# A Strassen SwiGLU stage: weight blocks loaded three column tiles ahead, with fewer pages for each tile

## Chip, cores and metric

The kernel runs on one core of one Trainium2 chip. The metric is the device time of one execution in microseconds (us), as the median of several runs of the same kernel. The profile is of one execution.

## The reference

One block of a diffusion backbone: 512 tokens of width 1024, and 256 context tokens. A mixing part (chunkwise retention and latent attention, merged by gates) is followed by a gated SwiGLU network of hidden width 2816. Everything is float32. The change lies in the first half of the network, where h is 512 x 1024 and w_gu 1024 x 5632:

```python
def _swiglu(h, w_gu, w_down):
    a, b = jnp.split(h @ w_gu, 2, axis=-1)
    return (jax.nn.silu(a) * b) @ w_down
```

## The kernel before, in words

**Numbers in two parts.** Every product in float32 is made of three matmuls (`mm3`, lines 121 to 123). Each operand is split into a high part, rounded by ACT (`split`, line 105), and a low part, the difference, which DVE makes (line 106).

**Tiles.** The hidden width is 22 tiles of 128 columns, each with a gate block and an up block of w_gu, 128 x 1024 each. Tiles 0 to 2 are computed plainly (`early_mm`). Tiles 3 to 21, 19 of them, go through the class `Hidden`, in Strassen's way: a 2 x 2 scheme over halves of the features and halves of the tokens with seven products instead of eight, `p1` to `p7`, in the order p1, p5, p2, p6, p3, p7, p4. A product is 12 matmuls of 128 x 128 weights on 256 columns, so a tile takes 84. The products p1, p6, p7 and p4 add up in one PSUM place, gy, and between them the running value is copied or added out: qz (line 1003, ACT), ub (line 1018, ACT), the sum of line 1027 (DVE), and lines 1031 and 1032 (DVE), which finish the tile. p5 and p3 add up in gz (line 1008, ACT, and line 1022, DVE), and p2 stands alone in gx (line 1013, DVE). Two neighbouring tiles, an even and an odd one, share a gy. The scheduler draws a piece of the next product between two products into gy.

**Operands of a tile.** `loads` brings four blocks. The first half of the up block goes twice into s13, by two transfers on SP's queue (lines 959, 960). The raw gate block goes into a ring of three raw buffers (`load`, line 110, SP). The second half of the up block, wgb, goes into a page (line 963, SP). Then POOL issues two accumulating transfers which add a further half to each half of s13 in memory (lines 964, 965). `sums` makes s24 from s13 and the raw block by two additions on DVE (lines 969, 970). Then the four splits follow: `split_a` (the raw block, into a ring of three weight buffers, "w"), `split_13`, `split_24` and `split_22` (into pages). There are 29 pages of 128 x 1024 words for everything.

**What sets the order.** Each engine and each queue works in order. The code is written step by step (the loop over f at the end of the stage) and a scheduler merges the steps into one order for each engine; waits follow from the data and from the buffers. In the loop, the loads of tile f+2 and its sums are written behind p6 of tile f, split_13 and split_24 of f+1 around p5 of f, and split_a of f+2 behind p3. Before the loop, the feature halves hx are combined into t1 to t4 (`combine`), each in a page of its own, and split as the moving operands T1 to T4. Behind the stage comes the projection with w_dn, whose raw blocks and splits use the same two rings.

Of the kernel before, what the change touches and what calls it, by code (L numbers as in the profile page):

```python
# [18 lines left out]
F32R = mybir.dt.float32r  # L19
BF16 = mybir.dt.bfloat16  # L20
AF = mybir.ActivationFunctionType
ALU = mybir.AluOpType
# [4 lines left out]
P = 128  # L27
# [36 lines left out]
def block(ctx: ExitStack, tc: tile.TileContext, xc, xtok, crow, wada, bada, w_rg, w_rv, w_rqk, w_kv, w_dq,  # L64
          w_gr, w_gm, w_ro, dec, ncol, w_qk, w_v, w_mo, w_out, lnrow, w_gu, w_dn, rtab, ktab, qtab, out):
    nc = tc.nc
    V, S, G, T = nc.vector, nc.scalar, nc.gpsimd, nc.tensor
# [3 lines left out]
    whl = ctx.enter_context(tc.tile_pool(name="whl", bufs=3))  # L71
# [10 lines left out]
    def nm(s):  # L82
        uid[0] += 1
        return f"{s}{uid[0]}"

    def page(shape, dt=F32, n="pg"):
        return pgp.tile(shape, dt, tag="pg", name=nm(n))

    def eight(shape, dt=F32, n="e8"):
        return e8p.tile(shape, dt, tag="e8", name=nm(n))  # L90

    def half(shape, dt=F32, n="hp"):
        return hpp.tile(shape, dt, tag="hp", name=nm(n))
# [4 lines left out]
    def bank(n="ps"):  # L98
        return pss.tile([P, 512], F32, tag="ps", name=nm(n))
# [4 lines left out]
    def split(h, l, src):  # L104
        S.copy(h, src)  # L105
        V.tensor_tensor(l, src, h.bitcast(F32), ALU.subtract)  # L106

    def load(ap, n):
        t = wraw.tile([P, 1024], F32, tag="wr", name=nm("wr"))
        nc.sync.dma_start(t[:, :n], ap)  # L110
        return t

    def weight(ap, n=1024):
        r = load(ap, n)
        w = whl.tile([P, 2, 1024], F32R, tag="w", name=nm("w"))
        split(w[:, 0, :n], w[:, 1, :n], r[:, :n])
        return w
# [55 lines left out]
    for ft in range(KT):  # L173
        if ft + 2 < KT:
            first_loads(ft + 2)
        bs, bh, r, xp = first[ft]
# [5 lines left out]
        h = eight([P, 2, NL], F32R, "hL")  # L182
# [5 lines left out]
        w = whl.tile([P, 2, 1024], F32R, tag="w", name=nm("w"))  # L188
        split(w[:, 0], w[:, 1], r)
        for n in range(8):  # L190
            c = slice(n * P, (n + 1) * P)
# [99 lines left out]
    def feat_mm(o, st, mv, ktn=KT):  # L291
        for k in range(ktn):
            mm3(o, st(k), mv(k), k == 0, k == ktn - 1)
# [232 lines left out]
    def run(g):  # L526
        for _ in g:
            pass
# [161 lines left out]
    for n in range(8):  # L690
        retention_out(n)
        if n == KN:
# [11 lines left out]
            sums = page([64, NL], n="sums")  # L704
# [9 lines left out]
    w = weight(w_v)  # L714
    m = row_max(0)
    vt = []
    for t in range(NTA):
# [4 lines left out]
        for f in range(2):  # L722
            if t < NTL:
                st = ck[f][:, 0, t * P:(t + 1) * P], ck[f][:, 1, t * P:(t + 1) * P]
            else:
                c = slice((t - NTL) * P, (t - NTL + 1) * P)
# [130 lines left out]
    hx, hb = {}, {}  # L857
# [69 lines left out]

    def combine(a, b, op, n):  # L930
        t = page([P, 4, 256], n=n)
        V.tensor_tensor(t, a, b, op)
        return t

    def moving(src, n, neg=False):
        a, b = eight([P, 4, 256], F32R, n + "h"), eight([P, 4, 256], F32R, n + "l")
        if neg:
            S.activation(a, src, AF.Copy, scale=-1.0)
            V.scalar_tensor_tensor(b, src, -1.0, a.bitcast(F32), ALU.mult, ALU.subtract)
        else:  # L940
            split(a, b, src)
        return a, b

    def product(o, st, mv, more=False):
        for k in range(4):
            c = slice(k * P, (k + 1) * P)
            mm3(o, (st[0][:, c], st[1][:, c]), (mv[0][:, k], mv[1][:, k]), k == 0 and not more, k == 3, more)

    class Hidden:
# [6 lines left out]
        def loads(self):  # L956
            ga, gb = w_gu[2 * self.f], w_gu[2 * self.f + 1]
            s = self.s13 = page([P, 2, 512], n="s13")
            nc.sync.dma_start(s[:, 0], gb[:, :512])
            nc.sync.dma_start(s[:, 1], gb[:, :512])  # L960
            self.a = load(ga, 1024)
            self.b = page([P, 512], n="wgb")
            nc.sync.dma_start(self.b, gb[:, 512:])
            G.dma_start(s[:, 0], gb[:, 512:], accum_op=ALU.add)  # L964
            G.dma_start(s[:, 1], ga[:, :512], accum_op=ALU.add)
# [8 lines left out]
            split(w[:, 0], w[:, 1], self.a)  # L974
            self.a11, self.a12 = [(w[:, 0, c], w[:, 1, c]) for c in (slice(0, 512), slice(512, 1024))]

        def halves(self, s, n):
            a, b = page([P, 2, 512], F32R, n + "h"), page([P, 2, 512], F32R, n + "l")
            split(a, b, s)
            return [(a[:, i], b[:, i]) for i in range(2)]  # L980

        def split_13(self):
            self.s1, self.s3 = self.halves(self.s13, "s13")

        def split_24(self):
            self.s2, self.s4 = self.halves(self.s24, "s24")

        def split_22(self):
            w = page([P, 2, 512], F32R, "a22")
# [35 lines left out]
        def p7(self):  # L1025
            product(self.y, self.s3, T3, True)
            V.tensor_tensor(self.ub[:, 1], self.y, self.qz[:, 1], ALU.add)

        def p4(self):
            product(self.y, self.a22, T4, True)  # L1030
            V.scalar_tensor_tensor(self.o[:, :256], self.y, -1.0, self.o[:, :256], ALU.mult, ALU.mult)
            V.scalar_tensor_tensor(self.o[:, 256:], self.ub[:, 1], -1.0, self.o[:, 256:], ALU.mult, ALU.mult)

    def steps(f, names):
        if f in hid:
            for n in names.split():
                getattr(hid[f], n)()

    ys = {}
    hid = {f: Hidden(f) for f in range(NEARLY, FT)}  # L1040

    def early_mm(f, tp):
        c = slice(tp * 256, tp * 256 + 256)
        pab = []
        for s in range(2):
            ps = bank("gu")
            feat_mm(ps[:, :256], wg[2 * f + s], lambda k: (hb[k // 4, tp][0][:, k % 4], hb[k // 4, tp][1][:, k % 4]))
            pab.append(ps[:, :256])
        sa = half([P, 256], n="sa")
        S.activation(sa, pab[0], AF.Silu)  # L1050
        V.tensor_tensor(tv[f // 2][:, f % 2, c], pab[1], sa, ALU.mult)
# [4 lines left out]
    F0 = NEARLY  # L1056
    for f in range(NEARLY):
        early_mm(f, 0)
    steps(F0, "loads")
    run(ln)  # L1060
    t1 = combine(hx[0, 0], hx[0, 1], ALU.subtract, "t1")
    q = combine(hx[1, 1], t1, ALU.add, "t2")
    early_mm(0, 1)
    T1 = moving(t1, "t1")
    steps(F0, "split_a split_13")
    early_mm(1, 1)
    T2 = moving(q, "t2", True)
    steps(F0, "sums split_24")
    steps(F0 + 1, "loads")
    for f in range(2, NEARLY):  # L1070
        early_mm(f, 1)
    T3 = moving(combine(hx[1, 1], hx[0, 1], ALU.subtract, "t3"), "t3")
    B11, B21, B22 = hb[0, 0], hb[1, 0], hb[1, 1]
    steps(F0, "p1")
    steps(F0 + 1, "split_a")
    steps(F0, "p5")
    T4 = moving(combine(q, hx[1, 0], ALU.subtract, "t4"), "t4")
    steps(F0, "p2 split_22 p6")
    steps(F0 + 1, "split_13 sums")
    steps(F0, "p3 p7")  # L1080
    steps(F0 + 1, "split_24")
    steps(F0 + 2, "loads")
    for f in range(F0 + 1, FT):
        steps(f, "p1")
        if f == F0 + 1:
            steps(f, "split_22")
            steps(f + 1, "sums split_a")
        steps(f + 1, "split_13")
        steps(f, "p5")
        steps(f + 1, "split_24")  # L1090
        steps(f, "p2")
        steps(f + 1, "split_22")
        steps(f, "p6")
        steps(f + 2, "loads sums")
        steps(f, "p3")
        steps(f + 2, "split_a")
        steps(f - 1, "p4")
        steps(f, "p7")
    steps(FT - 1, "p4")


# [39 lines left out]
    for k in range(FT):  # L1141
        w = weight(w_dn[k])
# [16 lines left out]
    for k in range(FT - NLATE):  # L1159
        w = weight(w_dn[k])  # L1160
# [34 lines left out]
    for k in range(FT - NLATE, FT):  # L1195
        r = load(w_dn[k], 1024)
        a = page([P, 1024], F32R, "wdh")
        b = page([P, 1024], F32R, "wdl")
# [119 lines left out]
```

## Time and profile before

| what | us |
|---|---|
| median of three runs | 1021.82 (1020.51 to 1023.26) |
| the profiled execution's own time | 1018.94 |
| its span in the profile | 1017.2 |
| the Strassen stage, tiles 3 to 21 | 226.3 |

The profile gives for each engine what it did and what it waited for. A timeline row reads: start, duration, engine and line, operation with its output and inputs, and in brackets the idle time before it with what ended it. "SPq" and "POOLq" are the instructions that issue transfers. PE is TensorE, DVE is VectorE, ACT is ScalarE. In the windows, an engine's busy time stands with its number of instructions in brackets, then the granted clock of TensorE as a share of the full one, the busy share of the DMA engines and the rate.

### The profile page before, as it was taken

The page shows a single profiled execution, that of the slowest core. Times are in us where ns is not written, and L with a number is a line of the kernel's source. Part 1 is how long each engine was busy: PE and PEld are TensorE (multiplying, and loading weights), DVE is VectorE, ACT ScalarE, POOL GpSimd, SP SyncE. Part 2 cuts the span into 40 slices and gives each one's busy share as a digit, 9 for nine tenths or more (in the row PEclk, how much of TensorE's full clock was granted, in tenths as well). Part 3 has the DMA queues.
Part 4 walks back from the last instruction along what each step waited for, and adds up shares of the span by engine and source line. Part 5 has one row for each costly group of instructions (what it writes and reads, how often), then busy time and mean ns, then how long its engine had stood idle before and what let it go on. Part 6 is the DMA issues. An engine that isn't in the chain of part 4 may idle for free. (4 is left out here: it accounts for less than half of the span.)

```text
span 1017.2 us, 13877 instructions
## 1 busy us (share of the span) xinstructions
PE 959.8 (94%) x5384; PEld 815.0 (80%) x5384; DVE 702.0 (69%) x1096; ACT 447.2 (44%) x686; POOL 76.8 (8%) x115
## 2 busy tenths in 40 slices
PE   5999999999999998999999989979899988999995
PEld 3888888888899786776766769978789988988884
DVE  6959877537753665788886867755667664794946
ACT  3344253323333531377676544434444442653341
POOL 0000100100011010000000001011112111000002
PEclk9999999999999999999999999999999998999998
DMA  9746511111034578510003576256667666576771
GB/s 356 310 132 233 211 63 42 42 57 47 22 116 144 164 218 248 125 42 22 1 2 124 181 218 206 82 142 148 162 175 179 157 164 146 187 248 196 216 227 44
DMA packets 52467, 147.49 MB, mean 145 GB/s; under 512 B 8113, under 2 KB 9265, under 8 KB 52401
## 3 DMA queue, kind: packets, MB, share of 16 engines
q1 hardware_dynamic: 39456, 123.62, 37.4%
q0 software_dynamic: 6112, 11.54, 7.2%
q10 hardware_dynamic: 6832, 11.45, 3.4%
q8 instruction: 42, 0.69, 0.3%
q14 instruction: 25, 0.20, 0.1%
HBM read 140.81 MB, written 4.20 MB: 143 GB/s over the span
## 5 line engine op out<-in xcount | busy, mean ns | idle before, releaser
L105 ACT CAST w<-wr 128x1024 fp32r<-128x1024 f32 (+2 forms) x137 | 141.4, 1033 | 194.4 <-PE wd L123 49.0
L106 DVE TENSOR_TENSOR w<-wr,w 128x1024 fp32r<-128x1024 f32 (+2 forms) x137 | 164.0, 1198 | 83.0 <-ACT w L105 82.9
L122 PE MATMUL wd<-w,tt 128*128 128x512 f32 (+1 forms) x163 | 61.0, 374 | 0.0
L121 PE MATMUL wd<-w,tt 128*128 128x512 f32 (+1 forms) x163 | 60.8, 374 | 0.0
L123 PE MATMUL wd<-w,tt 128*128 128x512 f32 (+1 forms) x163 | 60.8, 373 | 0.0
L121 PE MATMUL gt<-hL,w 128*128 128x512 f32 x128 | 50.9, 398 | 0.2 <-DVE ck L484 0.2
L122 PE MATMUL gt<-hL,w 128*128 128x512 f32 x128 | 50.7, 396 | 0.0
L123 PE MATMUL gt<-hL,w 128*128 128x512 f32 x128 | 50.7, 396 | 0.0
L149 DVE SCALAR_TENSOR_TENSOR junk<-wr,sc 128x1024 bf16<-128x1024 f32 x20 | 24.4, 1222 | 27.2 <-DMA wr<-in_wada_dram 26.5
L105 ACT CAST s13h<-s 128x1024 fp32r<-128x1024 f32 x19 | 19.9, 1047 | 51.8 <-DMA s<-in_w_gu_dram 51.8
L405 POOL TENSOR_SCALAR sm<-sm 128x1 f32<-128x1 f32 x18 | 8.8, 486 | 426.1 <-DVE sm L825 349.2
L106 DVE TENSOR_TENSOR s13l<-s,s13h 128x1024 fp32r<-128x1024 f32 x19 | 23.3, 1224 | 24.2 <-ACT s13h L105 24.2
L123 PEld LDWEIGHTS wd<-w,tt 128*128 128x128 f32 x163 | 30.7, 188 | 5.9
L121 PEld LDWEIGHTS wd<-w,tt 128*128 128x128 f32 x163 | 30.6, 188 | 5.9
L122 PEld LDWEIGHTS wd<-w,tt 128*128 128x128 f32 x163 | 30.6, 188 | 5.9
L106 DVE TENSOR_TENSOR pt<-ex,pt 128x512 fp32r<-128x512 f32 x48 | 30.7, 685 | 4.0 <-ACT pt L105 4.0
L614 DVE TENSOR_REDUCE sm<-sc 128x1 f32<-128x768 f32 x32 | 29.7, 952 | 2.4 <-PE sc L613 2.2
L969 DVE TENSOR_TENSOR s<-s,wr 128x512 f32<-128x512 f32 x19 | 13.1, 689 | 26.2 <-DMA s<-in_w_gu_dram 26.2
L964 POOL DMA_DIRECT2D s<-in_w_gu_dram x19 | 16.7, 876 | 189.5 <-DMA s<-in_w_gu_dram 64.1
L511 ACT ACTIVATE gate<-gt 128x512 f32<-128x512 f32 x16 | 9.6, 598 | 48.6 <-PE gt L123 48.6
L121 PE MATMUL gy<-t2h,s24h 128*128 128x256 f32 x76 | 22.5, 296 | 7.5 <-ACT qz L1003 7.5
L121 PEld LDWEIGHTS gt<-hL,w 128*128 128x128 f32 x128 | 24.1, 188 | 6.0 <-DVE ck L484 0.5
(438 smaller groups left out, 3144.1 us busy)
## 6 DMA issues: line engine op xcount, KB each, us to landing
wr<-in_w_dn_dram SPq DMA_DIRECT2D x44, 512.0 KB, 3.7
wr<-in_w_gu_dram SPq DMA_DIRECT2D x25, 512.0 KB, 3.5
wr<-in_wada_dram SPq DMA_DIRECT2D x20, 512.0 KB, 4.0
s<-in_w_gu_dram SPq DMA_DIRECT2D x38, 256.0 KB, 3.9
s<-in_w_gu_dram POOLq DMA_DIRECT2D x38, 256.0 KB, 4.5
wr<-in_w_out_dram SPq DMA_DIRECT2D x16, 512.0 KB, 4.3
ada_m<-in_wada_dram SPq DMA_DIRECT2D x12, 512.0 KB, 5.8
wgb<-in_w_gu_dram SPq DMA_DIRECT2D x19, 256.0 KB, 4.3
```

Of the source, the lines that this page charges most:

```text
L105: S.copy(h, src)
L106: V.tensor_tensor(l, src, h.bitcast(F32), ALU.subtract)
L121: T.matmul(o, st[0], mv[0], start=start, stop=False, skip_group_check=more)
L122: T.matmul(o, st[0], mv[1], start=False, stop=False, skip_group_check=more)
L123: T.matmul(o, st[1], mv[0], start=False, stop=stop, skip_group_check=more)
L149: V.scalar_tensor_tensor(junk, raw, 1.0, vec, ALU.mult, ALU.mult, accum_out=acc[:, b:b + 1])
L405: G.tensor_scalar(dst, src, scale, eps, ALU.mult, ALU.add)
L511: S.activation(dst[n // 2][:, n % 2], ps, AF.Sigmoid)
L614: V.tensor_reduce(mx[:, t:t + 1], ps.rearrange("p a b -> p (a b)")[:, :NA], AX.X, ALU.max)
L964: G.dma_start(s[:, 0], gb[:, 512:], accum_op=ALU.add)
L969: V.tensor_tensor(s[:, 0], self.s13[:, 0], self.a[:, :512], ALU.add)
```

## The change

- The loads of a tile are written three tiles ahead instead of two: those of f+3 behind p1 of f.
- `split_13` puts its two parts into the weight ring (name w13) instead of two pages. The ring keeps three buffers and now has two users.
- wgb of an even and an odd tile share one page.
- The differences t1 to t4 of the features are written over the halves hx that they are made from, so `combine` and its pages go.
- The steps stand in another order: split_24 of f+1 ahead of p2, split_13 of f+1 behind p2, sums of f+2 behind p6, split_a of f+2 behind p7, split_22 of a tile in its own round behind p5.

```diff
--- before.py
+++ after.py
@@ -927,11 +927,6 @@
 
 
 
-    def combine(a, b, op, n):
-        t = page([P, 4, 256], n=n)
-        V.tensor_tensor(t, a, b, op)
-        return t
-
     def moving(src, n, neg=False):
         a, b = eight([P, 4, 256], F32R, n + "h"), eight([P, 4, 256], F32R, n + "l")
         if neg:
@@ -959,7 +954,9 @@
             nc.sync.dma_start(s[:, 0], gb[:, :512])
             nc.sync.dma_start(s[:, 1], gb[:, :512])
             self.a = load(ga, 1024)
-            self.b = page([P, 512], n="wgb")
+            if self.f // 2 not in bs:
+                bs[self.f // 2] = page([P, 2, 512], n="wgb")
+            self.b = bs[self.f // 2][:, self.f % 2]
             nc.sync.dma_start(self.b, gb[:, 512:])
             G.dma_start(s[:, 0], gb[:, 512:], accum_op=ALU.add)
             G.dma_start(s[:, 1], ga[:, :512], accum_op=ALU.add)
@@ -974,16 +971,15 @@
             split(w[:, 0], w[:, 1], self.a)
             self.a11, self.a12 = [(w[:, 0, c], w[:, 1, c]) for c in (slice(0, 512), slice(512, 1024))]
 
-        def halves(self, s, n):
-            a, b = page([P, 2, 512], F32R, n + "h"), page([P, 2, 512], F32R, n + "l")
-            split(a, b, s)
-            return [(a[:, i], b[:, i]) for i in range(2)]
-
         def split_13(self):
-            self.s1, self.s3 = self.halves(self.s13, "s13")
+            w = whl.tile([P, 2, 1024], F32R, tag="w", name=nm("w13"))
+            split(w[:, 0], w[:, 1], self.s13.rearrange("p a b -> p (a b)"))
+            self.s1, self.s3 = [(w[:, 0, c], w[:, 1, c]) for c in (slice(0, 512), slice(512, 1024))]
 
         def split_24(self):
-            self.s2, self.s4 = self.halves(self.s24, "s24")
+            a, b = page([P, 2, 512], F32R, "s24h"), page([P, 2, 512], F32R, "s24l")
+            split(a, b, self.s24)
+            self.s2, self.s4 = [(a[:, i], b[:, i]) for i in range(2)]
 
         def split_22(self):
             w = page([P, 2, 512], F32R, "a22")
@@ -1036,7 +1032,7 @@
             for n in names.split():
                 getattr(hid[f], n)()
 
-    ys = {}
+    ys, bs = {}, {}
     hid = {f: Hidden(f) for f in range(NEARLY, FT)}
 
     def early_mm(f, tp):
@@ -1058,44 +1054,48 @@
         early_mm(f, 0)
     steps(F0, "loads")
     run(ln)
-    t1 = combine(hx[0, 0], hx[0, 1], ALU.subtract, "t1")
-    q = combine(hx[1, 1], t1, ALU.add, "t2")
+    t1, t3, q, t4 = hx[0, 0], hx[0, 1], hx[1, 1], hx[1, 0]
+    V.tensor_tensor(t1, hx[0, 0], hx[0, 1], ALU.subtract)
+    V.tensor_tensor(t3, hx[1, 1], hx[0, 1], ALU.subtract)
+    V.tensor_tensor(q, hx[1, 1], t1, ALU.add)
     early_mm(0, 1)
     T1 = moving(t1, "t1")
     steps(F0, "split_a split_13")
+    steps(F0 + 1, "loads")
     early_mm(1, 1)
     T2 = moving(q, "t2", True)
     steps(F0, "sums split_24")
-    steps(F0 + 1, "loads")
+    steps(F0 + 2, "loads")
     for f in range(2, NEARLY):
         early_mm(f, 1)
-    T3 = moving(combine(hx[1, 1], hx[0, 1], ALU.subtract, "t3"), "t3")
+    T3 = moving(t3, "t3")
+    V.tensor_tensor(t4, q, hx[1, 0], ALU.subtract)
     B11, B21, B22 = hb[0, 0], hb[1, 0], hb[1, 1]
     steps(F0, "p1")
+    steps(F0 + 3, "loads")
     steps(F0 + 1, "split_a")
-    steps(F0, "p5")
-    T4 = moving(combine(q, hx[1, 0], ALU.subtract, "t4"), "t4")
-    steps(F0, "p2 split_22 p6")
-    steps(F0 + 1, "split_13 sums")
+    steps(F0, "p5 p2 split_22 p6")
+    steps(F0 + 1, "sums")
+    T4 = moving(t4, "t4")
+    steps(F0 + 1, "split_13 split_24")
     steps(F0, "p3 p7")
-    steps(F0 + 1, "split_24")
-    steps(F0 + 2, "loads")
+    steps(F0 + 1, "split_22")
+    steps(F0 + 2, "sums split_a")
     for f in range(F0 + 1, FT):
         steps(f, "p1")
-        if f == F0 + 1:
+        steps(f + 3, "loads")
+        steps(f, "p5")
+        if f > F0 + 1:
             steps(f, "split_22")
-            steps(f + 1, "sums split_a")
-        steps(f + 1, "split_13")
-        steps(f, "p5")
         steps(f + 1, "split_24")
         steps(f, "p2")
-        steps(f + 1, "split_22")
+        steps(f + 1, "split_13")
         steps(f, "p6")
-        steps(f + 2, "loads sums")
+        steps(f + 2, "sums")
         steps(f, "p3")
-        steps(f + 2, "split_a")
         steps(f - 1, "p4")
         steps(f, "p7")
+        steps(f + 2, "split_a")
     steps(FT - 1, "p4")
```

The first place is SP's queue in the middle of the stage. s13 is the sum block of a tile, wr its raw gate block, wgb its second up half; before, the rows are these:

```order
L110 DMA wr1043_6232<-in_w_gu_dram 128x1024
L959 DMA s131012_5981<-in_w_gu_dram 128x512
L960 DMA s131012_5981<-in_w_gu_dram 128x512
L963 DMA wgb1014_5986<-in_w_gu_dram 128x512
L110 DMA wr1059_6357<-in_w_gu_dram 128x1024
L959 DMA s131028_6106<-in_w_gu_dram 128x512
L960 DMA s131028_6106<-in_w_gu_dram 128x512
L963 DMA wgb1030_6111<-in_w_gu_dram 128x512
L110 DMA wr1073_6480<-in_w_gu_dram 128x1024
L959 DMA s131042_6229<-in_w_gu_dram 128x512
L960 DMA s131042_6229<-in_w_gu_dram 128x512
```

and with the change:

```order
L110 DMA wr1013_6052<-in_w_gu_dram 128x1024
L110 DMA wr1025_6173<-in_w_gu_dram 128x1024
L954 DMA s131024_6170<-in_w_gu_dram 128x512
L955 DMA s131024_6170<-in_w_gu_dram 128x512
L960 DMA wgb1026_6175<-in_w_gu_dram 128x512 x2
L954 DMA s131039_6294<-in_w_gu_dram 128x512
L955 DMA s131039_6294<-in_w_gu_dram 128x512
L110 DMA wr1040_6297<-in_w_gu_dram 128x1024
L110 DMA wr1052_6418<-in_w_gu_dram 128x1024
L954 DMA s131051_6415<-in_w_gu_dram 128x512
```

Before, the raw block of a tile stands right ahead of the s13 loads of the tile two before it (wr1043 belongs to the same tile as s131042, in the last row but one). With the change the raw block and the s13 loads of one tile stand together (wr1025 and s131024), the wgb loads of two tiles follow each other, and the loads of two tiles stand side by side.

The second place is DVE's queue from the sum of p2 of an even tile to the sum of p7 of the same tile, on which p1 of the odd tile waits (L1027 before, L1023 with the change). Before:

```order
L1013 TENSOR_TENSOR tv1078_6534<-gx1085_6571,qz1079_6535 128x256
L1022 TENSOR_TENSOR tv1078_6534<-gz1082_6553,ub1087_6588 128x256
L106 TENSOR_TENSOR a221086_6585<-wgb1074_6482,a221086_6585 128x512
L1031 SCALAR_TENSOR_TENSOR tv1048_6286<-gy1047_6285,tv1048_6286 128x256
L1027 TENSOR_TENSOR ub1087_6588<-gy1077_6533,qz1079_6535 128x256
L1032 SCALAR_TENSOR_TENSOR tv1078_6534<-ub1087_6588,tv1078_6534 128x256
L969 TENSOR_TENSOR s241091_6611<-s131088_6602,wr1089_6605 128x512
L970 TENSOR_TENSOR s241091_6611<-s241091_6611,wr1089_6605 128x512
```

and with the change (the line numbers are four lower there, and three for the sums):

```order
L1009 TENSOR_TENSOR tv1091_6769<-gx1099_6813,qz1092_6770 128x256
L966 TENSOR_TENSOR s241102_6844<-s131078_6660,wr1079_6663 128x512
L106 TENSOR_TENSOR w131100_6827<-s131066_6539,w131100_6827 128x1024
L967 TENSOR_TENSOR s241102_6844<-s241102_6844,wr1079_6663 128x512
L106 TENSOR_TENSOR a221109_6928<-wgb1053_6420,a221109_6928 128x512
L1018 TENSOR_TENSOR tv1091_6769<-gz1095_6792,ub1101_6830 128x256
L106 TENSOR_TENSOR s24l1111_6932<-s241102_6844,s24h1110_6931 128x1024
L1027 SCALAR_TENSOR_TENSOR tv1064_6524<-gy1063_6523,tv1064_6524 128x256
L966 TENSOR_TENSOR s241115_6966<-s131093_6784,wr1094_6787 128x512
L1023 TENSOR_TENSOR ub1101_6830<-gy1090_6768,qz1092_6770 128x256
L967 TENSOR_TENSOR s241115_6966<-s241115_6966,wr1094_6787 128x512
```

The sum of p7 is the row whose output is ub1087, and ub1101 with the change. Before, the two additions for a later tile (L969, L970) stand behind it. With the change the first addition for the tile three further on (L966, s241115) stands ahead of it, and so do both additions for the tile before that one (s241102), with the splits w131100, a221109 and s24l1111. On TensorE, five matmuls of p5 of the odd tile stood between p7 of the even tile and p1 of the odd one; with the change there are eight.

## Rows read from the trace of the kernel before

**Rows 1.** The page: its first line, the span and the instructions of the execution.

```profile
span 1017.2 us, 13877 instructions
```

**Rows 2.** Windows: start:end, length, busy us by engine, PEclk, DMA share, GB/s.

```profile
659.30:885.60 226.30, 201.74 (x1604) 196.05 (x1603) 141.11 (x214) 99.12 (x160) 30.99 (x36) 0.98 0.64 162
760.00:780.00 20.00, 19.37 (x163) 19.15 (x162) 14.56 (x22) 9.74 (x15) 3.49 (x4) 1.00 0.73 183
850.00:859.00 9.00, 6.89 (x35) 6.89 (x36) 4.94 (x6) 4.86 (x8) 1.67 (x2) 0.62 0.52 164
```

**Rows 3.** The same window, instructions of gy, gz and gx alone (PE first).

```profile
659.30:885.60 226.30, 120.66 (x907) 113.19 (x907) 15.17 (x37) 14.00 (x38) 0.98 0.64 162
...
659.30:885.60 226.30, 64.34 (x456) 58.90 (x456) 7.91 (x19) 7.02 (x19) 0.98 0.64 162
...
659.30:885.60 226.30, 31.01 (x228) 29.11 (x228) 7.96 (x19) 0.98 0.64 162
```

**Rows 4.** Timeline: start, us, engine, line, operation [idle before, and releaser].

```profile
775.17 0.28 PE L122 MATMUL gy<-t3l,s13h 128*128 128x256 f32 x1
...
776.59 0.28 PE L122 MATMUL gz<-t1l,s13h 128*128 128x256 f32 x1
...
777.03 0.41 DVE L1027 TENSOR_TENSOR ub<-gy,qz 128x256 f32<-128x256 f32 x1
...
777.50 0.39 PE L121 MATMUL gy<-hbh,w 128*128 128x256 f32 x1 [0.63 <-DVE ub L1027]
```

**Rows 5.** Waits of PE in 659.3 to 885.6: us in total, times, longest.

```profile
PE gy L121 <- ACT qz L1003: 7.5, 4, 3.1
PE gy L121 <- ACT ub L1018: 6.0, 5, 1.7
PE gy L121 <- DVE ub L1027: 3.9, 4, 1.3
PE gz L121 <- ACT s13h L105: 3.5, 2, 3.1
PE gz L121 <- ACT qz L1008: 2.1, 2, 1.5
```

**Rows 6.** Waits of SP's queue in 659.3 to 885.6.

```profile
SPq L110 <- DVE s L970: 142.9, 16, 14.1
```

**Rows 7.** Timeline: one round of loads, and the first raw load of the count.

```profile
669.71 0.33 SPq L110 DMA_DIRECT2D wr<-in_w_gu_dram  x1
...
835.50 0.33 SPq L110 DMA_DIRECT2D wr<-in_w_dn_dram  x1
...
836.25 1.04 ACT L105 CAST s13h<-s 128x1024 fp32r<-128x1024 f32 x1 [5.59 <-DMA s<-in_w_gu_dram]
...
838.15 0.36 ACT L1003 COPY qz<-gy 128x256 f32<-128x256 f32 x1
...
838.57 0.38 PE L121 MATMUL gy<-t2h,s24h 128*128 128x256 f32 x1 [2.61 <-ACT qz L1003]
...
840.10 0.42 SPq L960 DMA_DIRECT2D s<-in_w_gu_dram  x1
...
843.44 1.22 POOL L965 DMA_DIRECT2D s<-in_w_gu_dram  x1
...
848.55 0.33 SPq L110 DMA_DIRECT2D wr<-in_w_dn_dram  x1
...
850.74 1.04 ACT L105 CAST s13h<-s 128x1024 fp32r<-128x1024 f32 x1 [7.64 <-DMA s<-in_w_gu_dram]
```

**Rows 8.** DMA issues on the page: count, KB each, median us to landing.

```profile
s<-in_w_gu_dram SPq DMA_DIRECT2D x38, 256.0 KB, 3.9
s<-in_w_gu_dram POOLq DMA_DIRECT2D x38, 256.0 KB, 4.5
```

**Rows 9.** DVE's groups in 700 to 880: busy us, mean ns, idle before.

```profile
L106 DVE TENSOR_TENSOR w<-wr,w 128x1024 fp32r<-128x1024 f32 x15 | 18.3, 1217 | 0.0
L969 DVE TENSOR_TENSOR s<-s,wr 128x512 f32<-128x512 f32 x15 | 10.4, 690 | 23.5 <-DMA s<-in_w_gu_dram 23.5
```

## The prediction

> **What bounds the kernel now.** I read the windows first, then the waits of TensorE, then the queue of SP, and last one round of loads in the timeline. The span is 1017.2 us [rows 1]. The changed stage runs from the first Strassen matmul of tile 3 to the last of tile 21, 659.30 to 885.60, so 226.3 us with 1604 matmuls [rows 2]. Of these, 907 + 456 + 228 = 1591 write gy, gz and gx [rows 3]; the 13 others are the first of the projection behind. Inside an undisturbed run the matmuls start 0.118 us apart: the rows at 775.17 and 776.59 are twelve matmuls apart, 1.42 us [rows 4]. So 1591 matmuls need 188.2 us, or 84 x 0.118 = 9.92 us a tile. The 13 others are 512 columns wide; at twice the spacing they take 3.1 us. That leaves 226.3 - 188.2 - 3.1 = **35.0 us in which TensorE is held up**, and this is all that the change can win there.
>
> Where are these 35.0 us? The five largest groups of TensorE's waits come to 7.5 + 6.0 + 3.9 + 3.5 + 2.1 = 23.0 us [rows 5]. All but one name a copy or sum that takes a product out of PSUM (lines 1003, 1008, 1018, 1027). The mean granted clock of the stage is 0.98, so about 0.02 x 226.3 = 4.5 us more; it falls to 0.62 in 850 to 859, right behind a pause of TensorE [rows 2]. The rest is small.
>
> The releasers named are quick instructions, though; the question is why they were late. The round in rows 7 tells it. TensorE starts p6 at 838.57 after 2.61 us idle, for the copy of line 1003. ACT starts that copy at 838.15, because the casts of that round stand ahead of it in its queue, and the first of them began at 836.25, after ACT had idled 5.59 us for the DMA of s13. So the sum block was late, and ACT, in order, took the evacuation down with it.
>
> Why was the block late? SP waits 142.9 us in the stage, 16 times, with the raw load (line 110) for the second addition of the sums, line 970 [rows 6]. The raw ring has three buffers, so the raw block of tile f+2 waits until tile f-1's is read; and in SP's order the two loads of s13 of tile f stand behind it. The raw load (here already one of w_dn) goes at 835.50, the second load of s13 at 840.10, the accumulating transfers are issued by POOL until 843.44, the cast behind them begins at 850.74, and the next raw load goes at 848.55 only [rows 7]. This is a closed loop, one turn for each tile. Added up from its rows: three issues on SP 0.33 + 0.33 + 0.42 (the first s13 load taken like the raw one), landing 3.9 [rows 8], POOL's issue 1.22 [rows 7], landing of the accumulate 4.5 [rows 8], two additions of 0.69 [rows 9]: 12.1 us. Measured it is (848.55 - 669.71) / 16 turns = **11.18 us** [rows 7], against the 9.92 that TensorE needs. The loop, not TensorE, sets the pace: 19 x (11.18 - 9.92) = 23.9 us, which is about the 23.0 of the waits.
>
> **The change, part by part.**
> Loads three tiles ahead. SP's raw load of tile f now waits for the ring to be read by split_a and the sums of f-3, and the s13 loads wait for pages freed by p3 and p4 of f-5 and f-6. In SP's new order the loads of a tile stand together. The turn thus goes over three tiles, with 12.1 us of transfers in it against some 2 x 9.92 = 19.8 us between the issue and the first use (line 966 of the same tile). It leaves about 8 us to spare. Every wait for the s13 DMA goes. What is late next is DVE, below. Can the queues carry it? A tile moves seven times 256 KB, 1.84 MB in 9.92 us, 185 GB/s; the stretch 760 to 780 had 183 GB/s with the DMA engines busy to 0.73 and TensorE 19.37 of 20 us [rows 2]. Yes.
>
> The raw split in the weight ring. The sums of s13 now take one of three ring buffers instead of two pages. Two users share the ring: split_13 of f+1 waits for p2 of f, split_a of f+2 for p7 of f. Both are needed only products later, so I take nothing in the stage; at the end, the first split of the next projection waits until the last p6 has read the ring. That cast and subtraction (about 1.0 + 1.22 [rows 9]) lie partly beside the last two products (2 x 12 x 0.118 = 2.8 us): bounds 0 and 2.2, I take 1.0.
>
> wgb in shared pages, differences in place. Neither adds an instruction in the loop. Pages per tile fall from 8 to 5.5, which is what lets three tiles be in flight. In place, t3 is made earlier than before: two more wide DVE operations stand among the splits ahead of p1 of tile 3. Bounds 0 and 2 x 1.22 = 2.4 by the nearest row [rows 9]; they have other matmuls of the early tiles over them, so I take 0.5. If that cover were gone, it would be 2.4.
>
> The new order on DVE. This is the term that stays. Products of one pair of tiles write the same gy, and p1 of the odd tile waits until DVE has added p7 of the even one (line 1023, before line 1027); the wait is 0.63 to TensorE in the row at 777.50, which starts 0.47 after the sum began at 777.03 [rows 4]. Now eight matmuls of p5 lie between p7 and p1, before it was five: 0.35 us more cover. But in front of line 1023 the queue holds, from p2's end: line 1009, line 966, w13l, 967, a22l, 1018, s24l, 1027, line 966 of the next tile, so 0.41 + 0.69 + 1.22 + 0.69 + 0.69 + 0.41 + 1.22 + 0.41 + 0.69 = 6.4 us by [rows 4, 9]. A matmul lasts 0.28, 0.16 beyond its slot [rows 4]; so, counted from p2's last slot, this is done at 6.6, and TensorE restarts 0.47 after line 1023's start, 7.1. TensorE itself comes to p1 after p6, p3, p4, p7 and 8 of p5, 56 x 0.118 = 6.6. The wait is 0.5 by full durations; back-to-back instructions on DVE overlap by up to a tenth, so the lower end is 0. I take 0.25, plus 0.1 for p7 of the odd tile behind the sum of p4: 0.35 for a pair, 9 pairs, **3.2 us**; bounds 0 and 5.4 (0.6 x 9).
>
> Sum: of the 35.0 us, 3.2 + 0.5 + 1.0 = 4.7 stay; 30.3 go. The profiled execution took 1018.94 us, so 988.6; the median of the runs, 1021.82, lies 2.9 above it, so **991 us** in their scale. If all 35.0 went it would be 983.9, or 986.8; I set the low end at 985.
>
> A rule against this. The rows show 3.9 and 4.5 us from issue to landing for 256 KB [rows 8], and 7.3 between the second POOL issue and the cast behind it [rows 7]. With these the turn is over 9.92. The Trainium skill, page "DMA: Bandwidth & Descriptors", section "Anatomy of one DMA — SWDGE (gpsimd) path", gives about 2.0 us plus bytes over 436 GB/s for such a transfer, so an estimate of 2.6 us; by it a turn would be 8.9 us, shorter than a tile's matmuls, the loads would hold nobody, and earlier loads would win nothing. The trace disagrees: the rows say 4.5 and the measurement decides.
>
> **The rivals.**
> (a) DVE becomes the bound. If one more 1024-wide half, w of split_a, falls in front of line 1023 in each pair, 1.22 us more are lost there: 9 x 1.22 = 11.0. For it: DVE is busy 14.56 of 20 us when TensorE runs full [rows 2], and is in order. Against: split_a comes behind line 1023 in its order. The gain is then 19.3 and the time 1002. Chance 0.13.
> (b) The loads are not the cause, or the loop only moves: the transfers land in a burst and the raw ring, still of three, keeps the pace at 11.18. A loop whose turn is short without contention, as reckoned from rows by less than 9.92, would be the same case. For it: the ring did not grow. Against: SP's 142.9 us wait is for line 970, which has a tile more time now. Time 1018 to 1022. Chance 0.06.
> (c) Slower. In DVE's new order line 966 of a tile three ahead stands in front of line 1023. A late accumulate would then hold the evacuation of p7, and TensorE, directly, and no longer ACT's copies alone. It decides when issue to landing passes some 20 us; the longest turn in rows, 835.50 to 850.74, is 15.2. Loads of two tiles now leave together, 3.7 MB; at the 183 GB/s of [rows 2] that is 20 us. To be slower it must cost more than 35.0 / 19 = 1.84 us a tile; at 2.4 it is 19 x 2.4 = 45.6, 10.6 more than now, 1032. Chance 0.03, as the queues had 0.27 of their time free in that stretch.
>
> **How the numbers follow.** The forecast has 0.78: 991, alone 985 to 997 (with the upper bounds 5.4 + 2.4 + 2.2 = 10.0 left in the stage, 25.0 go: 993.9, or 996.8). Case (a) adds 0.13 up to 1002. I give 985 to 1002, which leaves out (b), (c) and a little of either end. About 0.3% (3 us) is what a measurement of this kernel can tell from no change. Faster by more than that: 0.78 + 0.13 = 0.91; the same, case (b): 0.06; slower, (c): 0.03.
>
> **What would show it.** In the changed profile the stage should last about 196 us (193 without the 13 others) with a granted clock of 1.00. ACT's wait for the s13 DMA should be gone, raw loads on SP should go at 10 us spacing, and TensorE's waits should come to some 5 us, led by gy waiting for the sum of line 1023. If raw loads still go every 11 us, (b) is right; if gy waits for line 1023 over 1 us a pair, (a); if line 966 idles for the DMA, (c). Should the stage fall as forecast but the span not, a stage behind it lost what this one won.

## The result, and the profile after

The changed kernel takes 994.56 us (median of four runs, 991.36 to 995.30) against 1021.38 us (median of four). The ratio of the runs is 0.9729, 95% interval 0.9703 to 0.9755; that of the two medians is 0.9737. The forecast was 991 us, in a range of 985 to 1002. Measured again later beside the kernel before (e10), the same kernel took 991.79 against 1019.27, 0.9732 (0.9706 to 0.9759). Two of the four executions of experiment e1 below, its profiled one among them, took 2400.73 and 1334.25 us for a reason that nothing here shows; its ratio is from the other two, and e5 repeats the kernel for a profile.

The profiled execution took 995.01 us with a span of 993.0. The windows of the stage, from its first full product to its last, and of its middle (columns as in [rows 2]):

```profile
663.90:860.40 196.50, 193.78 (x1600) 190.21 (x1599) 138.51 (x211) 103.71 (x159) 29.66 (x34) 1.00 0.66 174
700.00:820.00 120.00, 119.65 (x991) 117.59 (x990) 86.46 (x130) 62.83 (x95) 21.16 (x24) 1.00 0.71 182
```

In the middle TensorE is busy 119.65 of 120 us at a granted clock of 1.00. The kernel before has there 108.32 and 888 matmuls instead of 991:

```profile
700.00:820.00 120.00, 108.32 (x888) 105.58 (x887) 79.37 (x120) 54.78 (x86) 19.79 (x23) 1.00 0.69 170
```

The waits of the stage, TensorE's first, then the two that answer to the s13 DMA and to SP's raw load [rows 5, 6]:

```profile
PE gy L121 <- DVE ub L1023: 2.2, 1, 2.2
```

```profile
DVE s L966 <- DMA s<-in_w_gu_dram: 2.0, 1, 2.0
```

```profile
SPq L110 <- DVE w L106: 92.7, 10, 10.6
SPq L110 <- DVE tv L1028: 46.1, 8, 9.4
...
SPq L110 <- DVE s L967: 3.9, 1, 3.9
```

Of the five groups of [rows 5], 23.0 us together, one wait of 2.2 us is left. ACT waits for the s13 DMA nowhere in the stage now, DVE once. SP waits for the ring still, but for split_a's subtraction ("DVE w") and not for the second addition. The row of line 1028 is the same wait under another name: at 707.13 the raw load goes right behind the end of that subtraction (705.88 + 1.22), and line 1028 had just begun beside it. How the raw loads follow each other shows in SP's timeline; a row with x2 holds the loads of two tiles:

```profile
707.13 11.03 SPq L110 DMA_DIRECT2D wr<-in_w_gu_dram  x2
...
727.47 11.08 SPq L110 DMA_DIRECT2D wr<-in_w_gu_dram  x2
...
788.59 11.01 SPq L110 DMA_DIRECT2D wr<-in_w_gu_dram  x2
```

From 707.13 to 788.59 are four pairs of tiles, 81.46 us: **10.18 us a tile**, against 11.18 before [rows 7] and the 9.92 of the matmuls. The lead itself is the time from a tile's first s13 load to its first addition, here of tile 12:

```profile
718.20 0.42 SPq L954 DMA_DIRECT2D s<-in_w_gu_dram  x1
```

```profile
739.93 0.68 DVE L966 TENSOR_TENSOR s<-s,wr 128x512 f32<-128x512 f32 x1
```

The addition starts 21.7 us behind the load and waits for nothing. From tile 8 on this lead is 21.5 us or more. In the kernel before, DVE was ready for the addition 3.6 to 11.0 us behind the load in tiles 6 to 21, and had to wait in 12 of these 16.

Where the rest stands, two places show. The first is at the start, tile 7's load (timeline, columns as in [rows 4]; then its landing in the DMA view, and the window):

```profile
666.07 0.42 SPq L954 DMA_DIRECT2D s<-in_w_gu_dram  x1
```

```profile
676.36 0.87 POOL L961 DMA_DIRECT2D s<-in_w_gu_dram  x1 [9.20 <-PE gx L123]
```

```profile
683.86 0.69 DVE L966 TENSOR_TENSOR s<-s,wr 128x512 f32<-128x512 f32 x1 [2.03 <-DMA s<-in_w_gu_dram]
684.47 0.42 DVE L1023 TENSOR_TENSOR ub<-gy,qz 128x256 f32<-128x256 f32 x1
...
684.94 0.39 PE L121 MATMUL gy<-hbh,w 128*128 128x256 f32 x1 [2.18 <-DVE ub L1023]
```

```profile
s<-in_w_gu_dram SPq DMA_DIRECT2D x2, 256.0 KB, 10.3
```

```profile
660.00:685.00 25.00, 22.82 (x195) 22.62 (x193) 20.21 (x30) 13.95 (x21) 7.05 (x8) 1.00 0.95 256
```

Its s13 load is issued at 666.07, right behind the raw load, which had waited for the ring (the raw block of tile 4). The DMA view of 664 to 667 gives 10.3 us from issue to landing for it, so POOL issues the accumulate at 676.36 only (the row names PE, which happened to end then), and the addition of line 966 starts behind its landing at 683.86: 10.3 and 7.5 us for transfers that take 3.9 and 4.5 in [rows 8]. In 660 to 685, where the loads of several tiles leave close together, the DMA engines are busy 0.95 of the time, against 0.59 in the kernel before; that this crowd makes the landings late is argued, no run here spreads the loads. Tile 7 has 15.8 us of lead and not the 21.5 of the loop. The addition has waited 2.03 us; the sum of p7 (line 1023) stands behind it on DVE, ready by then, and p1 of the odd tile behind that, 2.18 us. The second place recurs in every pair of tiles; here 806 to 807:

```profile
805.86 0.42 DVE L1027 SCALAR_TENSOR_TENSOR tv<-gy,tv 128x256 f32<-128x256 f32 x1
...
806.19 0.68 DVE L966 TENSOR_TENSOR s<-s,wr 128x512 f32<-128x512 f32 x1
...
806.79 0.41 DVE L1023 TENSOR_TENSOR ub<-gy,qz 128x256 f32<-128x256 f32 x1
...
807.26 0.19 PEld L121 LDWEIGHTS gy<-hbh,w 128*128 128x128 f32 x1 [0.33 <-DVE ub L1023]
```

No DMA is late here. Line 1027, line 966 and line 1023 follow each other without a pause, and p1's weights wait 0.33 us for the end of this queue.

The stage by kernel, from the trace of one execution of each. The matmuls of the projection that fall into it (12 in the kernel before, 7 in the changed one) take 0.234 us each and are taken off in the third column; the last column is the time at which the first early matmul of the network starts, that is, the length of everything ahead.

| kernel | stage | without the projection | ahead of it |
|---|---|---|---|
| before | 226.4 | 223.6 | 621.7 |
| changed | 196.5 | 194.8 | 626.3 |
| e2 two tiles ahead | 225.4 | 223.7 | 625.6 |
| e3 before, third add | 277.0 | 276.8 | 625.5 |
| e4 changed, third add | 202.4 | 200.8 | 622.8 |
| e5 before, three ahead | 202.2 | 199.4 | 622.9 |
| e6 changed, four raw buffers | 196.6 | 195.0 | 618.7 |
| e7 before, four raw buffers | 225.7 | 223.9 | 616.3 |
| e8 changed, s13 in pages | 194.6 | 193.0 | 622.9 |
| e9 before, three ahead, early start | 193.5 | 190.7 | 623.6 |
| e10 changed, again | 196.6 | 195.0 | 624.0 |
| e11 e8 with four raw buffers | 194.6 | 193.0 | 618.1 |
| e12 changed, own wgb pages | 199.9 | 198.5 | 622.2 |

### The profile page after: what moved, and what is told of

It is laid out like the page before. It is cut to its first block, busy times and chain, and to the rows that moved or that the text cites. A ratio compares the mean times of both kernels' runs of the same rounds, so it can differ in the third digit from the quotient of the medians.

```text
span 993.0 us, 13863 instructions
## 1 busy us (share of the span) xinstructions
PE 957.0 (96%) x5384; PEld 812.9 (82%) x5384; DVE 701.6 (71%) x1096; ACT 451.7 (45%) x686; POOL 76.0 (8%) x115
## 4 chain that ended last, share of the span: by engine, by line
PE 79%; DVE 7%; DMA 7%; ACT 3%; issue 3%; POOL 1%; POOLq 0%; SPq 0%; ACTq 0%; DVEq 0%
PE wd L122 4%; PE wd L123 4%; PE wd L121 4%; PE gy L121 3%; DMA wr<-in_wada_dram 3%; PE gy L123 3%; PE gy L122 3%; PE gt L121 2%; PE gt L123 2%; PE gt L122 2%; DMA wr<-in_w_out_dram 2%; DVE w L106 2%; PE rva L121 2%; PE rva L123 2%; PE rva L122 1%
## 5 line engine op out<-in xcount | busy, mean ns | idle before, releaser
L121 PE MATMUL ro<-gtd,w 128*128 128x512 f32 x64 | 26.0, 406 | 3.1 <-ACT w L105 3.1
L121 PEld LDWEIGHTS gt<-hL,w 128*128 128x128 f32 x128 | 24.1, 188 | 6.0 <-DVE ck L484 0.5
L123 PEld LDWEIGHTS gt<-hL,w 128*128 128x128 f32 x128 | 24.1, 188 | 5.8
L122 PEld LDWEIGHTS gt<-hL,w 128*128 128x128 f32 x128 | 24.1, 188 | 5.5
L642 ACT ACTIVATE ex<-st 128x512 f32<-128x512 f32 x48 | 27.1, 601 | 2.6 <-PE st L123 2.4
L105 ACT CAST w<-s 128x1024 fp32r<-128x1024 f32 x19 | 20.0, 1051 | 18.3 <-PE gx L123 18.3
```

What stands on the lines that cost most here:

```text
L121: T.matmul(o, st[0], mv[0], start=start, stop=False, skip_group_check=more)
L122: T.matmul(o, st[0], mv[1], start=False, stop=False, skip_group_check=more)
L123: T.matmul(o, st[1], mv[0], start=False, stop=stop, skip_group_check=more)
L642: S.activation(ex, ps, AF.Exp, scale=SSC)
```

## The experiments

The times of e3, e4, e5, e7, e8 and e12 are of one execution each, so that for these the stage of the table tells more than the time.

**e1 and e5: the lead alone.** In the kernel before, only the loads move:

```diff
     steps(F0 + 2, "loads")
+    steps(F0 + 3, "loads")
...
         steps(f, "p1")
+        steps(f + 3, "loads")
...
-        steps(f + 2, "loads sums")
+        steps(f + 2, "sums")
```

> The kernel before with one part of the change: the loads of a tile written three tiles ahead. Pages, ring users, differences and all other steps stay as before (8 pages a tile). In SP's order the raw block and the s13 loads of a tile then stand together. Theory T (the turn through the raw ring, closed by SP's order, set the pace): the tie is gone, raw loads go about every 10.3 us, and the time falls to 997 to 1008. Theory P (the saved pages are what lets loads run ahead): s13 loads wait for pages instead, and the time stays at 1012 to 1030. Theory O (the new order of the splits and sums behind the evacuations did it): 1018 to 1025.

Measured: 0.9807 of before (0.9777 to 0.9838), 997.79 and 998.69 us, two executions alone. Theory T holds, P and O fall. For the rest:

> The same kernel as e1 (the kernel before, loads three tiles ahead, 8 pages a tile), once more for a profile. Theory T with pages as the second limit: stage 203 to 209 us instead of 226, the s13 loads on SP (lines 959, 960) now wait for pages, by several us in most tiles, and the raw loads wait behind them; TensorE still waits for ACT behind the s13 casts in some tiles, about 10 us together. If the pages hold nothing: stage 195 to 198, as in the changed kernel, and the rest of its loss stands elsewhere.

The time is 996.17 us, and the stage is 199.4 without the projection. The waits of SP and of TensorE in it:

```profile
SPq L959 <- DVE a L106: 31.8, 4, 10.2
SPq L959 <- PE gz L123: 26.8, 4, 12.7
...
SPq L959 <- PE gy L123: 17.9, 3, 8.4
```

```profile
PE gz L121 <- ACT s13h L105: 5.0, 1, 5.0
PE gz L121 <- ACT qz L1008: 1.4, 1, 1.4
```

Pages do hold the s13 loads, 76.5 us in these three groups, as expected. But nobody waits behind them: TensorE's waits are single ones and lie at the start (5.0 us at 685.1, 1.4 at 667.1); in 700 to 820 it is busy without a break:

```profile
700.00:820.00 120.00, 120.00 (x1005) 119.01 (x1005) 85.74 (x131) 61.48 (x95) 19.36 (x22) 1.00 0.68 176
```

So a load that waits for a page and still lands in time costs nothing; the "about 10 us together" that I expected in some tiles was wrong.

**e2: everything but the lead.**

```diff
-        steps(f + 3, "loads")
...
-        steps(f + 2, "sums")
+        steps(f + 2, "loads sums")
```

(and the start alike).

> The changed kernel with its loads two tiles ahead again, in their old place behind p6; fewer pages, the ring with two users and the new order of splits stay. In SP's order the raw load of tile f+2 stands ahead of the s13 loads of tile f once more. Theory T: raw loads every 11 us or so, ACT and DVE wait for the s13 DMA in most tiles, time 1008 to 1022. Theories P and O: 992 to 1000.

Measured: 1020.35 us, 1.0016 of before (1.0002 to 1.0031): all of the gain is gone. The waits of DVE, of TensorE and of SP, and the first and the last of 16 raw loads on SP:

```profile
DVE s L966 <- DMA s<-in_w_gu_dram: 29.5, 13, 3.8
```

```profile
PE gy L121 <- DVE ub L1023: 18.7, 8, 3.0
```

```profile
SPq L110 <- DVE w L106: 131.2, 14, 12.0
```

```profile
686.41 0.33 SPq L110 DMA_DIRECT2D wr<-in_w_gu_dram  x1
...
868.40 0.33 SPq L110 DMA_DIRECT2D wr<-in_w_dn_dram  x1
```

Fifteen turns in 181.99 us are 12.13 us each. The loop is back, and a little longer than before; the raw load waits here for split_a's subtraction, which stands behind the sums. The late block now holds TensorE in another way: not through casts ahead of copies on ACT but through line 966 ahead of line 1023 on DVE, 18.7 us. That is the mechanism of my rival (c), at work where the lead is missing.

**e3 and e4: a third accumulating transfer in both kernels.** It adds the same half once more, so the output's values change.

```diff
             G.dma_start(s[:, 0], gb[:, 512:], accum_op=ALU.add)
+            G.dma_start(s[:, 0], gb[:, 512:], accum_op=ALU.add)
```

> The kernel before with a third accumulating transfer for each tile (the first half of s13 is added to twice, so the values of the output change; the matmuls are the same in number). It costs POOL about 1.2 us and a landing of about 4.5 us in the chain of each tile. Theory T: a turn is already longer than the matmuls of a tile, so all of it is seen: 5 to 6 us in each of some 17 turns, 85 to 100 us, time 1100 to 1125. If transfers were hidden and TensorE held by orders on ACT and DVE (O): within 10 us of 1021.

> The same third accumulating transfer for each tile in the changed kernel (the values of the output change likewise). Theory T with some 8 us to spare from issue to first use: the loop hides it, apart from the start, where line 966 of tile 7 already waited 2.0 us; time 995 to 1004. If there is no such slack (rival c: the first addition stands ahead of the sum of p7 and a late transfer holds TensorE): each tile loses 2 us or more, time over 1030.

Before: 1077.31 us, 58 more than the 1018.84 of the kernel before beside it; the stage is 53.2 us longer. The raw loads at both ends of 15 turns:

```profile
674.75 0.33 SPq L110 DMA_DIRECT2D wr<-in_w_gu_dram  x1
...
894.45 0.33 SPq L110 DMA_DIRECT2D wr<-in_w_dn_dram  x1
```

A turn is 14.65 us, 3.5 more. I had priced it at 5 to 6: the direction holds, the size does not. POOL's rows of one tile show why (the line added is 965; the transfer for the other half moved to 966):

```profile
767.73 0.87 POOL L964 DMA_DIRECT2D s<-in_w_gu_dram  x1 [10.91 <-PE gx L123]
768.44 1.06 POOL L966 DMA_DIRECT2D s<-in_w_gu_dram  x1
771.87 0.88 POOL L965 DMA_DIRECT2D s<-in_w_gu_dram  x1 [2.36 <-DMA s<-in_w_gu_dram]
```

The third transfer waits until the first, which writes the same bytes, has landed. The transfer for the other half is under way in that time, so the third is issued only 3.43 us behind it. After: 998.82 us, the stage 6.0 us longer, and that at the start (line 967 is line 966 of the changed kernel, one lower by the line added):

```profile
674.51 0.69 DVE L967 TENSOR_TENSOR s<-s,wr 128x512 f32<-128x512 f32 x1 [7.93 <-DMA s<-in_w_gu_dram]
...
678.54 0.58 PE L121 MATMUL gy<-t2h,s24h 128*128 128x256 f32 x1 [5.88 <-ACT qz L1000]
```

```profile
678.00:690.00 12.00, 11.46 (x78) 11.46 (x79) 10.80 (x17) 7.65 (x13) 2.00 (x3) 0.78 0.90 231
...
700.00:820.00 120.00, 119.63 (x991) 117.56 (x990) 85.53 (x129) 62.22 (x94) 31.10 (x35) 1.00 0.88 209
```

Line 967 waits 7.93 us for its transfer and p6 5.88 us behind it, where the changed kernel had one wait of 2.2; behind that pause the granted clock is 0.78 for some 12 us. In the loop the same extra transfer costs nothing: 991 matmuls in 700 to 820, as many as in the changed kernel. So the loop has at least the 3.5 us to spare that e3 shows, and the start has nothing.

**e7 and e6: a fourth raw buffer**, in the kernel before and in the changed one.

```diff
-NPG = 29
+NPG = 28
...
-    wraw = ctx.enter_context(tc.tile_pool(name="wraw", bufs=3))
+    wraw = ctx.enter_context(tc.tile_pool(name="wraw", bufs=4))
```

> The kernel before with four raw buffers and 28 pages. In its SP order the raw load then stands one tile further ahead: that of f+3 ahead of the s13 loads of f, and it waits for the sums of f-1 as before. Theory T (the tie is made by the order on SP, not by the size of the ring): the turn stays, raw loads every 11 to 12 us, stage 222 to 232. Rival R (three raw buffers are too few): stage under 212.

> The changed kernel with four raw buffers instead of three, and 28 pages instead of 29. In its start tile 7's raw load waits for split_a of tile 4, its s13 loads stand behind that in SP's queue, and line 966 is 2.0 us late, ahead of the sum of p7. Theory T: with a fourth buffer the raw load goes a tile earlier, the pause of 2.46 us at the start goes, stage 194 instead of 196.5, time 2 us under the changed kernel (0.2%, at the edge of what can be told from the time; the pause tells). Rival: the lost page is worth more than the buffer: s13 loads wait longer, 2 to 10 us slower.

Before with four: the stage is 223.9, as with three, and SP waits for the same instruction [rows 6]:

```profile
SPq L110 <- DVE s L970: 137.0, 16, 13.7
```

The raw loads go every 11.40 us (665.10 to 847.52, 16 turns). With the longer ring the scheduler moves the raw load one tile further ahead in SP's order, and the tie stays: theory T holds, R falls. A longer ring with SP's order left as it was, and without the page that it cost, was not tried. The time is nevertheless 1013.11, 5 us less; those 5 us lie ahead of the stage, see below. Changed with four: 986.29 us, 0.9671 (0.9639 to 0.9703), but the stage is 195.0, no shorter. The two waits at its start are

```profile
PE gy L121 <- ACT qz L999: 1.4, 1, 1.4
PE gy L121 <- DVE ub L1023: 0.6, 1, 0.6
```

so the pause of tile 7 shrank from 2.2 to 0.6 us as expected, and one of 1.4 us came elsewhere. Neither the theory nor its rival had the gain ahead of the stage.

**e8, e12: the parts that save pages**, undone one by one in the changed kernel: split_13 in two pages, and a page for each wgb.

```diff
-            w = whl.tile([P, 2, 1024], F32R, tag="w", name=nm("w13"))
-            split(w[:, 0], w[:, 1], self.s13.rearrange("p a b -> p (a b)"))
+            a, b = page([P, 2, 512], F32R, "s13h"), page([P, 2, 512], F32R, "s13l")
+            split(a, b, self.s13)
...
```

```diff
-            if self.f // 2 not in bs:
-                bs[self.f // 2] = page([P, 2, 512], n="wgb")
-            self.b = bs[self.f // 2][:, self.f % 2]
+            self.b = page([P, 512], n="wgb")
```

> The changed kernel with the two parts of split_13 in two pages again, not in the weight ring: 7.5 pages a tile, one user of the ring; all else stays, three tiles ahead too. Theory T with pages as the second limit: between e5 and the changed kernel, stage 198 to 206, with s13 loads waiting for pages freed a tile later. If pages are no limit: 196 to 197.

> The changed kernel with a page of its own for each wgb (6 pages a tile instead of 5.5). If pages are no limit once loads are three tiles ahead (as e8 with 7.5 says): stage without the projection's matmuls 193 to 196.5, as the changed kernel. If sharing is what keeps the loads going: 198 or more.

e8: the stage is 193.0, shorter than the changed kernel's, not longer. Pages are no limit here, and the shared ring costs 1.8 us. e12: 198.5, above what I expected. It has a longer pause at the start, and a window with a lower clock behind it:

```profile
PE gy L121 <- DVE ub L1021: 3.2, 1, 3.2
```

```profile
678.00:695.00 17.00, 13.81 (x92) 13.47 (x92) 7.76 (x12) 5.56 (x9) 2.85 (x4) 0.80 0.64 141
700.00:855.00 155.00, 154.54 (x1281) 152.13 (x1280) 108.48 (x165) 79.89 (x123) 21.20 (x24) 1.00 0.62 167
```

In 700 to 855 TensorE is busy 154.54 us with 1281 matmuls, the changed kernel in e10 154.44 with 1274: the loop is untouched. The loss is the start's, and its pause is that of the changed kernel, longer: the same addition (line 964 here) waits 3.06 us for its transfer instead of 2.03.

```profile
680.68 0.69 DVE L964 TENSOR_TENSOR s<-s,wr 128x512 f32<-128x512 f32 x1 [3.06 <-DMA s<-in_w_gu_dram]
```

Why the transfer lands later there I have not settled.

**e9: the lead alone, with an early start.** As e5, but the loads of tiles 4, 5 and 6 are written in the start where the changed kernel has them. Nothing else of the change is in it.

> The kernel before with nothing but its loads moved: three tiles ahead in the loop, and in the start behind the steps where the changed kernel has them. Eight pages a tile, the old step order, the ring with one user, combine pages: all as before. Theory L (the lead of the loads is all of the gain; e5 lost only in its start): the 5.3 us pause of e5 at its start shrinks, stage without the projection's matmuls 193 to 197 against 194.8 of the changed kernel, time 0.970 to 0.978 of before. If pages or the step order are needed for the rest: 199 as in e5, 0.980.

Measured: 988.07 us (987.84 to 989.26), 0.9698 (0.9672 to 0.9725); stage 190.7. That beats the whole change, whose time beside it is 991.79 (e10), and the stage is shorter than I expected. TensorE's one wait in it:

```profile
PE gy L121 <- DVE ub L1027: 0.5, 1, 0.5
```

**e10 and e11: the changed kernel beside the best version** (e8 with e6's four raw buffers).

> The changed kernel itself, unaltered, beside the others on this chip. Theory S (the 3.5 us by which it fell short of the forecast are mostly the part ahead of the stage, which differs from one execution to the next by some us whatever the kernel): the part ahead of the first early matmul of the stage, 626.3 us in the profile so far, lies somewhere in 621 to 626, and the stage is again 194 to 196.5. If the change costs those 4 us itself: 626 again and 995.

> The changed kernel with split_13 in pages (e8) and four raw buffers with 28 pages (e6) together, the version that should beat both. By e8 the stage is 193.0 without the projection's matmuls; by e6 and e7 the part ahead of it is about 5 us shorter with four raw buffers. Theory: both add, time 983 to 987, under e6's 986.3. If a page less hurts now that eight are not shared with the ring: stage over 196, time 988 or more.

e10: 991.79 us (991.09 to 993.00); stage 195.0, the part ahead 624.0. e11: 984.38 us (979.95 to 984.80), 0.9650 (0.9623 to 0.9677): stage 193.0, the part ahead 618.1; both gains add. It is faster than both kernels. e9 with four raw buffers may be faster still; it was not tried.

## Why the prediction was right, point by point

- **The bound.** Right. The stage lost 28.7 us without the projection's matmuls (223.6 to 194.8), forecast 30.3. e5 and e9 against e2 show that the lead of the loads alone makes it (24.2 us of the stage in e5, 32.9 in e9) and that without the lead nothing is left; e3 against e4 show that a transfer's time is on the path before and hidden after; e7 shows that a larger ring does not help while a raw load stands ahead of the s13 loads of an earlier tile. By the rule that I weighed (the Trainium skill, page "DMA: Bandwidth & Descriptors", section "Anatomy of one DMA — SWDGE (gpsimd) path") I let the loads hold nobody. That does not hold here: before, the accumulates landed after 4.5 us [rows 8], and in the changed kernel, where two tiles' loads leave together, after 6.1:

```profile
s<-in_w_gu_dram SPq DMA_DIRECT2D x38, 256.0 KB, 4.3
s<-in_w_gu_dram POOLq DMA_DIRECT2D x38, 256.0 KB, 6.1
```

The working was wrong too. This section of the Trainium skill gives its fit for POOL's path alone, and I had put its 2.6 us in place of SP's 3.9 as well. For the accumulate alone the sum is 12.1 - 1.9 = 10.2 us, an estimate, which is still over 9.92: the rule was no rival.
- **"Pages per tile fall from 8 to 5.5, which is what lets three tiles be in flight."** Wrong. With 8 pages e9 keeps three tiles in flight and has the shortest stage. The pages saved are not what the gain rests on.
- **"I take nothing in the stage" for the shared weight ring.** Wrong by 1.8 to 2.0 us (e8 against the changed kernel and e10).
- **"I take 0.5" for the start.** Mis-sized: 2.2 us of wait. I had placed it in the differences made in place; it is tile 7's load, issued behind a wait for the ring and landing late among the crowded loads of the start. It is rival (c), which I had as a danger to the whole loop, and it came true in one tile of short lead. The crowd alone does not make the pause: in e9 the DMA engines are as busy there (0.94 in 657 to 682), and no wait is over 0.5 us.
- **"0.35 for a pair, 3.2 us."** Mis-sized: 20.37 us a pair against 168 x 0.1183 = 19.88, so 0.49, and 4.4 for nine. It is within the bounds of 0 and 5.4 and has the causes that I named: p1 loses about 0.3 us a pair, forecast 0.25, and p7 of the odd tile, behind the sum of p4, about 0.2, forecast 0.1. e9, with the old order of steps, has a good deal less of it: a stage of 190.7 is 2.5 us above the 188.2 of the matmuls, all causes together.
- **"I take 1.0" at the end.** Mis-sized: one interval of 0.51 instead of 0.234 between two matmuls of the projection (855.65 to 856.17), 0.3 us.
- **The sum.** 188.2 + 4.4 + 2.3 + 0.3 = 195.2, measured 194.8; forecast 192.9. The 2.3 is the pause of the start, two matmuls 2.46 us apart instead of 0.12.
- **What lies around the stage.** I took it as unchanged. In the profiled executions it is 4.6 us longer ahead of the stage (621.74 to 626.31), which makes up most of the distance from the 988.6 that I forecast for the profiled execution to its 995.01. It is not the change: in ten executions with three raw buffers, of both kernels and their variants, that part holds the same 2890 matmuls in the same order and takes 621.7 to 626.3, 625.5 for a variant of the kernel before (e3) and 622.8 for one of the changed kernel (e4). What differs is the granted clock behind short pauses. The 4.6 us come mostly in three steps, at 390 to 400 (a clock of 1.00 before, 0.83 with the change), at 552 to 556 (1.00 and 0.71) and in this window, the kernel before first:

```profile
603.00:613.00 10.00, 10.00 (x46) 8.13 (x46) 6.05 (x9) 4.63 (x5) 0.73 (x2) 0.87 0.89 288
```

```profile
603.00:613.00 10.00, 8.24 (x23) 6.17 (x24) 7.21 (x10) 6.28 (x6) 2.28 (x4) 0.66 0.78 238
```

Behind the stage it is 1.1 us longer, because five matmuls of the projection, 1.2 us, that stood in the stage before come behind it now. That the later 991.79 (e10) is so near the 991 of the forecast is in part luck: the stage is 195.0 there too, and not 192.9.
- **Rival (a)**, DVE as the bound, did not come: 0.49 us a pair instead of 1.57. **Rival (b)** fell with e1. Its remark that the ring did not grow was no argument: in e7 the ring grows and the stage stays.

## What to carry to other kernels

When an engine waits for a quick instruction, ask what stood ahead of that one, and go on until you reach a queue that waits for its own output: here SP's queue, where a load for a later tile waited ahead of a load for an earlier one. Here more lead, that is another order on that queue, broke the loop, and a larger ring with the raw load ahead as before did not. Try the smallest edit by itself first: here the lead alone, with the start's loads moved along, was worth more than the change with its four further parts (988.07 against 991.79 us).

## What was not expected

- A fourth raw buffer, bought with one page, shortens the part ahead of the stage, which I had not looked at: 616.3, 618.7 and 618.1 us (e7, e6, e11), under all ten executions with three (621.7 to 626.3). Which stage of that part it helps was not looked into.
- The same part, the same instructions in the same order, takes up to 4.6 us more from one execution to the next, by stretches of lower clock (0.66 against 0.87 in the window above). A stage's gain is then better read from the stage than from the time: 28.7 us in the stage, 26.8 and 27.5 between the medians, measured twice.
- An addition that waits for a DMA, set by a scheduler ahead of a sum that TensorE waits for, turns a late load into a TensorE wait at once (2.03 us of one, 2.18 of the other at the start; in e2 29.5 and 18.7 us in total).
